# A two-layer decoder trunk on one core: two more expert tiles fetched ahead of a pass, and five gathered rows moved between passes

## The chip, the cores and the metric

The kernel runs on one core of one Trainium2 chip. Its time is the device time of one execution in microseconds (us); the median of three runs of the kernel before is 1489.36 us (1488.99 to 1492.16). Five engines work side by side, each through its own list of instructions in order: PE (matrix products), DVE (vector work), ACT (activations, copies, casts), POOL (here casts, and the issue of gathers) and SP (the issue of plain loads). All loads and gathers are carried by the core's 16 DMA engines.

## The reference

Two layers. Each has a mixer (layer 0: block-sparse attention and retention side by side; layer 1: a short gated convolution), and after it the expert retrieval "PEER", around which this change turns. The sequence has 256 tokens of 1024 numbers; u and v hold 16384 experts of 1024 numbers per layer.

```python
def peer(xn, w_q, sub_keys, u, v):
    ...
    q = (t @ w_q).reshape(n_tok, PEER_HEADS, 2, PEER_DKEY // 2)
    sc = jnp.einsum('thpd,hpnd->thpn', q, sub_keys).astype(jnp.float32)
    s1, i1 = lax.top_k(sc[:, :, 0], PEER_TOPK)
    s2, i2 = lax.top_k(sc[:, :, 1], PEER_TOPK)
    ...
    top_s, pos = lax.top_k(cand, PEER_TOPK)
    eidx = jnp.take_along_axis(cidx, pos, axis=-1)
    gate = jax.nn.softmax(top_s, axis=-1).astype(xn.dtype)
    ...
        hid = jax.nn.gelu(jnp.einsum('td,thkd->thk', tc, u[ec]), approximate=False)
        return jnp.einsum('thk,thkd->td', gc * hid, v[ec])

def reference(...):
    h = x
    for layer in range(DEPTH):
        xn = rmsnorm(h, norm_mix[layer])
        ...
        h = h + peer(rmsnorm(h, norm_ffn[layer]), peer_w_q[layer], peer_sub_keys[layer],
                     peer_u[layer], peer_v[layer])
    return rmsnorm(h, final_norm)
```

Each token has 8 heads with 16 experts each, 128 experts in all.

## The kernel before

**Two ways for two groups of tokens.** The first 96 tokens (`TG`) are served by gathering: for each of their 128 experts the row of u, and later the row of v, is fetched from memory by index. Since a gathered row-set spans 128 partitions and 96 of them are taken by a token each, the other 32 carry further experts of the same tokens, so that 96 row-sets (`STEPS`) of u and 96 of v are enough; the text calls a row-set of 128 x 1024 numbers a "row". The other 160 tokens (`TD`) are served densely: all 128 tiles of u (128 experts each) are multiplied with them, the result is passed through gelu, multiplied by a gate matrix G that is zero where an expert was not chosen, and multiplied with all 128 tiles of v. A row and a tile both have 512 KB.

**Stages of `peer`.** The queries (loop over `f`, 16 tiles of wq, L1260); the pass over u (loop over `i`, 128 tiles, L1388, products in `dense_u`); the pass over v (L1466). The top-16 selections go from the pump, a list of small DVE jobs that is drained a little after each query and each tile of u. When it is empty, the indices are transposed (`idx_tr`), and G is made in 40 groups of four tokens (`onehots`, `shared`, `g_mm`, `g_put`) between the products of u; from then on each tile's result is multiplied by the groups that are done (L1403), and `g_put` multiplies what had been computed before.

**Loads.** `Stream` loads the weights in the order of their use into eight buffers (`RAW`), each load as soon as the tile that had the buffer is used up; in the pass over v every second load is issued by ACT, all others by SP. `PRE` names 22 of the 128 tiles of u that do not go through the stream: the key is the tile's number, the value says which memory it is loaded into. 0 to 10 is the region of `HG` (the dense result, of which the rows of the first tiles are not written yet), 11 to 13 the three accumulators of the gather, 14 to 19 buffers that the queries leave (`uhi`, `ulo`, `one`, `xb`), and 20 and 21 that of the keys (`ko`). `fetch` issues such a load on SP: the 14 of `early` one after each query from the second on (L1277), the 8 of `early_u` one after each tile of u from the second on (L1392).

**The gather.** `Gather.issue` starts gathers on POOL (L975) as long as there is a free row buffer and the index is known: two buffers (`grow`) from the start, four more (`rows`) from `widen`, after the last query. The indices of the first third of the rows come from `places(0)`, those of the others from `places(1)`. `step` is called after each tile: it adds `ga.rate` to a credit, and for each whole credit consumes one row on DVE (L985: product with the token and sum, for u; L1002: multiply and add, for v) and issues the next gather. So the rate lays down in the program how many rows are consumed beside each tile:

```python
                ga.rate = (0.9 if 8 <= i < 46 else 0.6) if gst["g"] < 0 else (UPTO[l] - ga.c) / (NK - CALM - i) if i < NK - CALM else 0.6
                if i < NK - QUIET:
                    ga.step()
```

`gst["g"]` is below 0 until the transposition is done. `UPTO` is the number of rows (of 192 in a layer) that are to be consumed 11 tiles before the end of the pass over u; the others are spread over the pass over v. After each 32 rows of u their 32 columns of `hid` are passed through gelu on ACT (L991) and multiplied by their gates on DVE (L992), some rows later (`self.later`).

**The pass over v.** Of its 128 tiles 95 (`SPL`) are split in two parts, by a cast on ACT (L1378) and a subtraction on DVE (L1385), and multiplied with a split result (L1501, L1503); the other 33 are used whole (L1497).

The lists of the engines are fixed when the program is built; nothing is reordered on the chip, and an instruction that waits holds up what stands behind it on its engine.

Of the kernel before, what the change touches and what calls it, by code (L numbers as in the profile page):

```python
# [14 lines left out]
AF = mybir.ActivationFunctionType  # L15
OP = mybir.AluOpType
# [12 lines left out]
NK = 128  # L29
# [8 lines left out]
STEPS = TG  # L38
# [4 lines left out]
GT = 4  # L43
UNIT = 2.0 ** 15
SCR = 11 * D
UPTO = (112, 110)
SPL = [i for i in range(NK) if i % 2 or i % 4 == 0 and i > 0]
CODE = 64.0
WHOLE = 1.5 * 2.0 ** 23
PRE = {5 * k: k for k in range(11)} | {23: 20, 43: 21, 58: 14, 64: 15, 70: 11, 76: 16, 82: 18, 88: 12, 94: 17, 100: 13, 106: 19}  # L50
AHEAD = 3
QUIET = 4
CALM = 11
# [141 lines left out]
def trunk_kernel(ctx, tc, x, small, cst, mcst, ew_in, ew_out, ow_in, ow_out, wq, keys, pu, pv, pun, gains, out):  # L195
# [54 lines left out]
    def nm(s):  # L250
        uid[0] += 1
        return f"{s}{uid[0]}"
# [685 lines left out]
    class Gather:  # L938
# [9 lines left out]
        def __init__(self, pool):  # L948
            few = pool.tile([P, ROWS, D], F32, tag="grow", name=nm("grow"))
            self.rows = [few[:, i, :] for i in range(ROWS)]  # L950
            self.acc = [pool.tile([P, D], F32, tag=f"gacc{q}", name=nm("gacc")) for q in range(3)]
            self.hid = pool.tile([P, STEPS], F32, tag="ghid", name=nm("ghid"))
            self.known = 0
            self.rate = 0.0
            self.i = 0
            self.c = 0
            self.credit = 0.0
            self.later = {}
# [8 lines left out]

        def issue(self):

            while (self.i < self.TOTAL and (self.i < self.known or self.known == STEPS)  # L970
                   and self.i < self.c + len(self.rows)):
                s_ = self.i
                self.i += 1
                table = pun if s_ < STEPS else pv.rearrange("l i p d -> (l i p) d")
                gp.indirect_dma_start(self.row(s_), None, table,  # L975
                                      bass.IndirectOffsetOnAxis(IG[:, 0, s_ % STEPS:s_ % STEPS + 1].bitcast(U32), 0))

        def consume(self):
            s_ = self.c
            r = self.row(s_)  # L980
            j = s_ % STEPS
            q = j // SUB
            w = self.hid[:, j:j + 1]
            if s_ < STEPS:
                v.scalar_tensor_tensor(r, r, 1.0, XG[:, q % 2, :], op0=OP.mult, op1=OP.mult, accum_out=w)  # L985
                if s_ == SUB - 1:
                    gp.dma_start(XG[TG:, 0, :], XG[2 * SUB:TG, 0, :])
                if j % SUB == SUB - 1:
                    w = self.hid[:, q * SUB:(q + 1) * SUB]
                    g = IG[:, 1, q * SUB:(q + 1) * SUB]  # L990
                    self.later[s_ + 2] = lambda: act.activation(w, w, AF.Gelu)  # L991
                    self.later[s_ + 4] = lambda: v.tensor_tensor(w, w, g, OP.mult)  # L992
            elif j % SUB == 0:
                so_far = self.acc[q - 1] if q else h[:, 0, :]
                v.scalar_tensor_tensor(self.acc[q][:TG], r[:TG], w[:TG], so_far[:TG], op0=OP.mult, op1=OP.add)
                v.tensor_scalar(self.acc[q][TG:], r[TG:], w[TG:], None, op0=OP.mult)
                if q:
                    self.part(q - 1)
                if q == 2:
                    self.later[s_ + 8] = self.fold  # L1000
            else:
                v.scalar_tensor_tensor(self.acc[q], r, w, self.acc[q], op0=OP.mult, op1=OP.add)  # L1002
            self.later.pop(s_, lambda: None)()
            self.c += 1
# [17 lines left out]
    def peer(l, before, norm):  # L1022
        with tc.tile_pool(name=nm("hg"), bufs=1) as hp:
# [45 lines left out]
            def fetch(i):  # L1069

                k = PRE[i]
                if k < 11:
                    t = [flat[:, k * D:(k + 1) * D]]
                elif k < 14:
                    t = [ga.acc[k - 11]]
                elif 14 < k < 18:
                    t = [st.hi_pool.tile([P, D], F32R, tag="hi", name=nm("uhi")).bitcast(F32)]
                elif k > 19:  # L1080
                    if k == 20:
                        there["ko"] = new_ko().rearrange("p (a d) -> p a d", a=2)
                    t = [there["ko"][:, k - 20, :]]
                elif k == 18:
                    t = [Xb.rearrange("p k s -> p (k s)").bitcast(F32)]
                else:
                    n = 1 if k == 14 else 2
                    t = [st.lo_pool.tile([P, D], BF16, tag="lo", name=nm("ulo")).bitcast(F32) for _ in range(n)]
                    t += [one] * (2 - n)
                n = D // len(t)  # L1090
                for j, p in enumerate(t):
                    nc.sync.dma_start(p, pu[l, i][:, j * n:(j + 1) * n])
                there[i] = [p[:, c:c + P] for p in t for c in range(0, n, P)]

            there = {}
            early = [i for i in sorted(PRE) if PRE[i] < 14]
            early_u = [i for i in sorted(PRE) if PRE[i] >= 14]
            early_u = early_u[2:] + early_u[:2]
            pump = Pump()

# [154 lines left out]
            def chain(th, hf):  # L1255
                pump.add((1.0, stage2_build(th, hf)))
                pump.add(*[(2.2, stage2_top(th, a, a + 2)) for a in range(hf * HH, (hf + 1) * HH, 2)])
                pump.add(*extract(th, hf))

            for f in range(NPAIR):  # L1260
                if f == 0:
                    pair = u_pair(xv["x2"], Xb, before.tail)
                ps = pair[f] if f < 2 else u_tile(xv["x2"], Xb)
                act.copy(qT[f % 2], ps[:, :S])
                if f == 1:
                    rows = before.rows()
                if 1 < f < 6:
                    rows[f - 2]()
                if f:
                    scores(f - 1)  # L1270
                    pump.add((1.35, stage1(0, f - 1, f)))
                    if f <= HH * 2:
                        pump.add((1.35, stage1(1, f - 1, f)))
                    if f == HH * 2:
                        chain(0, 0)
                        pump.add((0.6, lambda: places(0)))
                    if early:  # L1277
                        fetch(early.pop(0))
                pump.run(3.2)
# [79 lines left out]
            def dense_u(i):  # L1359
                if i in PRE:  # L1360
                    w = there.pop(i)
                else:
                    t = st.next()
                    w = [t[:, k * P:(k + 1) * P] for k in range(ND)]
                ps = acc_tile(i % 4, nm("hid")) if i % 4 < 2 else hid_tile(nm("hid"))
                for k in range(ND):
                    pe.matmul(ps[:, :TD], w[k], XF[:, k, :], start=k == 0, stop=k == ND - 1)  # L1367
                    if k == ND // 2 - 1:
                        slot(i)
                return ps  # L1370
# [16 lines left out]
            first = st.nu + NK - len(PRE)  # L1387
            for i in range(NK):  # L1388
                ps = dense_u(i)
                if i == 0:  # L1390
                    after_first()
                elif early_u:  # L1392
                    fetch(early_u.pop(0))
                if i == NK - 1:
                    gst["rate"] = 1.0
                    while gst["g"] < NG:
                        slot(i)
                T = max(gst["g"], 0) * GT
                if T < TD:
                    act.activation(HG[:, i, T:], ps[:, T:TD], AF.Gelu)  # L1400
                if T > 0:
                    act.activation(ps[:, :T], ps[:, :T], AF.Gelu)
                    v.tensor_tensor(HG[:, i, :T], ps[:, :T], HG[:, i, :T], OP.mult)  # L1403
                slot(i + 1)
                if gst["g"] < 0:
                    if i == first_late - 2:
                        pump.flush()
                    if pump.q:
                        pump.run(1.4)
                    else:  # L1410
                        gst["g"] = 0
                        gst["rate"] = NG / (2.0 * (NK - 10 - i))
                        gst["credit"] = -0.6
                        xv["gate"] = new_ko(F16)
                        for g in range(3):
                            onehots(g)
                        todo += [0, 1]
                        shared()
                        shared()
                ga.rate = (0.9 if 8 <= i < 46 else 0.6) if gst["g"] < 0 else (UPTO[l] - ga.c) / (NK - CALM - i) if i < NK - CALM else 0.6  # L1420
                if i < NK - QUIET:
                    ga.step()
                elif i in (NK - QUIET, NK - QUIET + 2):
                    weight_parts(i - NK + QUIET + 1)
# [151 lines left out]
```

## Time and profile before

| | us |
|---|---|
| median of three runs | 1489.36 |
| the profiled execution, whole | 1490.58 |
| its span, first to last instruction | 1488.80 |
| around the span (difference) | 1.78 |
| layer 0: first query's products begin | 128.18 |
| layer 0: first tile of u begins | 182.53 |
| layer 0: first tile of v begins | 489.45 |
| layer 1: first tile of u begins | 907.24 |

| engine | busy, share of the span |
|---|---|
| PE (products) | 97% |
| PE (weight loads) | 90% |
| DVE | 84% |
| ACT | 51% |
| POOL | 50% |

Reading it: a stage's table gives, for a stretch of the span, each engine's busy time with its number of instructions, the clock that was granted to PE, the mean share in which the 16 DMA engines were busy (1.0 is full), and GB/s. In a list of waits, "A <- B: 10.9, 13, 1.5" says that A stood idle for B for 10.9 us in 13 waits, the longest 1.5. In a timeline a row has its start, its length, the engine and the line, what it writes and reads, how many instructions were merged, and in brackets the idle time before it and what ended it. In a table of groups stand busy time and mean ns of one, then the idle time before them. PE's busy time holds its pipelined products from begin to end, so a full PE is not PE at its peak. For products of u there are two instructions per 128 x 128 block, 16 per tile.

### The profile page before, as it was taken

What the parts mean: (1) busy time and instruction counts of PE and PEld (TensorE: products, weight loads), DVE (VectorE), ACT (ScalarE), POOL (GpSimd) and SP (SyncE); (2) the same over time, 40 slices, a digit from 0 to 9 for tenths busy, and PEclk for the clock granted to TensorE, in tenths of its full rate; (3) what the DMA queues carried; (4) which work ended last, traced back from release to release, by engine and by line L of the source; (5) the groups of instructions that cost most, each with busy time, mean ns of one, the idle gap of its engine ahead of it and who ended that gap; (6) DMA issues with size and microseconds to landing.
All of it is one profiled execution on the core that took longest, in us unless ns stands there. A gap on an engine that the chain in (4) does not pass through costs nothing.

```text
span 1488.8 us, 30108 instructions
## 1 busy us (share of the span) xinstructions
PE 1438.1 (97%) x11184; PEld 1334.8 (90%) x11184; DVE 1246.5 (84%) x2467; ACT 761.3 (51%) x1825; POOL 744.9 (50%) x513
## 2 busy tenths in 40 slices
PE   9999999999999999999989999999999999999997
PEld 5667999999999998889889799999999999988886
DVE  5637999879999788888876589996899978888888
ACT  6556511258875454445564463212888745454544
POOL 6754545546667243345335374453566643443532
PEclk9999999999999999999999999999999999999999
DMA  8545899999999999999966478999999999999995
GB/s 322 199 145 203 311 378 409 395 409 408 405 402 396 394 400 405 406 394 404 409 242 230 169 277 326 407 408 396 408 405 401 399 397 407 399 408 409 398 406 228
DMA packets 147618, 532.80 MB, mean 358 GB/s; under 512 B 16976, under 2 KB 17360, under 8 KB 147472
## 3 DMA queue, kind: packets, MB, share of 16 engines
q1 hardware_dynamic: 72288, 258.43, 44.9%
q0 software_dynamic: 56608, 204.81, 35.1%
q10 hardware_dynamic: 18576, 67.64, 11.5%
q8 instruction: 88, 1.44, 0.4%
q14 instruction: 58, 0.48, 0.1%
HBM read 528.40 MB, written 1.05 MB: 356 GB/s over the span
## 4 chain that ended last, share of the span: by engine, by line
PE 54%; issue 17%; POOL 11%; DMA 9%; DVE 7%; ACT 2%; POOLq 0%; DVEq 0%; ACTq 0%; SPq 0%
PE hid L1367 30%; POOL rows L975 7%; PE hid L261 5%; DMA raw<-pu 4%; DMA raw<-pv 3%; POOL grow L975 3%; PE hid L267 2%; PE G L1327 2%; DMA rows<-pv,ig 2%; PE ea L295 2%; PE vo L1501 2%; PE ea L294 2%; PE ea L293 2%; DVE gacc L1002 1%; PE vo L1497 1%
## 5 line engine op out<-in xcount | busy, mean ns | idle before, releaser
L1367 PE MATMUL hid<-xf,raw 128*128 128x160 f32 x3392 | 487.4, 301 | 7.3 <-DMA raw<-pu 4.6
L1367 PEld LDWEIGHTS hid<-xf,raw 128*128 128x128 f32 x3392 | 467.1, 191 | 10.5 <-issue 5.6
L1378 ACT CAST vhi<-raw 128x1024 fp32r<-128x1024 f32 x190 | 198.5, 1046 | 266.1 <-DMA raw<-pv 218.9
L975 POOL DMA_INDIRECT rows<-pv,ig x128 | 192.5, 1504 | 209.2 <-DVE gacc L1002 180.0
L1385 DVE TENSOR_TENSOR vlo<-raw,vhi 128x1024 bf16<-128x1024 f32 x190 | 231.9, 1223 | 77.4 <-ACT vhi L1378 69.1
L1501 PE MATMUL vo<-ko,vhi 128*128 128x320 f32 x1520 | 270.5, 320 | 24.5 <-DVE ko L1460 23.5
L1501 PEld LDWEIGHTS vo<-ko,vhi 128*128 128x128 f32 x1520 | 224.3, 188 | 33.8 <-DVE ko L1460 32.5
L975 POOL DMA_INDIRECT rows<-pun,ig x128 | 170.7, 1334 | 136.0 <-DVE rows L985 63.2
L151 POOL TENSOR_TENSOR lo<-raw,hi 128x1024 bf16<-128x1024 f32 x70 | 167.9, 2408 | 85.7 <-ACT hi L149 82.8
L985 DVE SCALAR_TENSOR_TENSOR rows<-rows,xg 128x1024 f32<-128x1024 f32 x128 | 155.5, 1220 | 22.5 <-DMA rows<-pun,ig 22.4
L1400 ACT ACTIVATE hg<-hid 128x160 f32<-128x160 f32 (+14 forms) x240 | 62.7, 265 | 199.1 <-PE hid L1367 199.0
L1002 DVE SCALAR_TENSOR_TENSOR gacc<-rows,ghid,gacc 128x1024 f32<-128x1024 f32 x124 | 158.8, 1281 | 4.7 <-DMA rows<-pv,ig 3.9
L975 POOL DMA_INDIRECT grow<-pv,ig x64 | 99.7, 1558 | 122.8 <-DVE gacc L1002 110.9
L1497 PE MATMUL vo<-hg,raw 128*128 128x160 f32 x1056 | 157.3, 302 | 1.0 <-DVE hg L1403 1.0
L1497 PEld LDWEIGHTS vo<-hg,raw 128*128 128x128 f32 x1056 | 145.5, 190 | 1.4 <-DVE hg L1403 1.4
L1503 PE MATMUL vo<-hb,vlo 128*128 128x160 bf16 x1520 | 138.1, 234 | 2.1 <-DVE vlo L1385 2.1
L1317 ACT ACTIVATE ko<-ko,idxT 128x128 f16<-128x128 f16 x320 | 101.8, 390 | 51.1 <-DVE ko L1303 50.9
L1503 PEld LDWEIGHTS <-vlo 128*128 128x128 bf16 x1520 | 100.5, 98 | 22.1 <-DVE vlo L1385 3.1
L975 POOL DMA_INDIRECT grow<-pun,ig x64 | 81.3, 1270 | 77.6 <-DVE grow L985 43.3
L149 ACT CAST hi<-raw 128x1024 fp32r<-128x1024 f32 x100 | 102.8, 1046 | 30.0 <-PE hid L261 18.5
L261 PE MATMUL hid<-x,hi 128*128 128x256 f32 x800 | 107.4, 287 | 0.2 <-DVE cg L912 0.2
L1320 ACT ACTIVATE ko<-ko,idxT 128x128 f16<-128x128 f16 x320 | 101.1, 388 | 0.0
(251 smaller groups left out, 2097.2 us busy)
## 6 DMA issues: line engine op xcount, KB each, us to landing
raw<-pu SPq DMA_DIRECT2D x212, 512.0 KB, 7.9
raw<-pv SPq DMA_DIRECT2D x128, 512.0 KB, 8.9
raw<-pv ACTq DMA_DIRECT2D x128, 512.0 KB, 8.0
raw<-wq SPq DMA_DIRECT2D x32, 512.0 KB, 3.9
raw<-ew_in SPq DMA_DIRECT2D x28, 512.0 KB, 4.5
raw<-ow_in SPq DMA_DIRECT2D x24, 512.0 KB, 5.3
hg<-pu SPq DMA_DIRECT2D x22, 512.0 KB, 5.1
raw<-ew_out SPq DMA_DIRECT2D x8, 512.0 KB, 3.1
```

The source lines that it names most:

```text
L149: self.nc.scalar.copy(hi, t)
L151: eng.tensor_tensor(lo, t, hi.bitcast(F32), OP.subtract)
L261: pe.matmul(ps[:, :S], hi[:, k * P:(k + 1) * P], A2[:, k, s_, :], start=k == 0 and s_ == 0, stop=False)
L975: gp.indirect_dma_start(self.row(s_), None, table, bass.IndirectOffsetOnAxis(IG[:, 0, s_ % STEPS:s_ % STEPS + 1].bitcast(U32), 0))
L985: v.scalar_tensor_tensor(r, r, 1.0, XG[:, q % 2, :], op0=OP.mult, op1=OP.mult, accum_out=w)
L1002: v.scalar_tensor_tensor(self.acc[q], r, w, self.acc[q], op0=OP.mult, op1=OP.add)
L1367: pe.matmul(ps[:, :TD], w[k], XF[:, k, :], start=k == 0, stop=k == ND - 1)
L1378: act.copy(whi[j], raw)
L1385: v.tensor_tensor(wlo[j], raw, whi[j].bitcast(F32), OP.subtract)
L1497: pe.matmul(vo[b][:, :TD], w[:, b * P:(b + 1) * P], HG[:, i, :], stop=False, **m)
L1501: pe.matmul(vo[b][:, :2 * TD], hi[:, b * P:(b + 1) * P], hs, stop=i == NK - 1, **m)
L1503: pe.matmul(vo[b][:, :TD], lo[:, b * P:(b + 1) * P], hb, stop=i == NK - 1, **m)
```

## The change

Five edits, alike in both layers.

1. `PRE` gets two more tiles: tile 1 and tile 2 of u, with the values 22 and 23, are loaded into the first two row buffers of the gather (`ga.rows[0]` and `[1]`, which are `grow`). They leave the stream, and belong to `early`, which now has 16 loads; three of these (tiles 0, 1, 2) are asked for ahead of the first query, the other 13 one after each query from the second on.
2. `Gather.held`: no gather is issued until tile 2 of u is done, since the first two row buffers hold tiles 1 and 2 until then.
3. The loads of `early_u` are all issued after the first tile of u, not one after each tile.
4. `UPTO` is 117 and 115 in place of 112 and 110, and the rate in the stretch of tiles 8 to 45 is 0.93 in place of 0.9.
5. Gelu and gate product of a third of the rows stand 12 and 16 rows after its last row, not 2 and 4.

```diff
@@ -43,11 +43,11 @@
 GT = 4
 UNIT = 2.0 ** 15
 SCR = 11 * D
-UPTO = (112, 110)
+UPTO = (117, 115)
 SPL = [i for i in range(NK) if i % 2 or i % 4 == 0 and i > 0]
 CODE = 64.0
 WHOLE = 1.5 * 2.0 ** 23
-PRE = {5 * k: k for k in range(11)} | {23: 20, 43: 21, 58: 14, 64: 15, 70: 11, 76: 16, 82: 18, 88: 12, 94: 17, 100: 13, 106: 19}
+PRE = {5 * k: k for k in range(11)} | {1: 22, 2: 23, 23: 20, 43: 21, 58: 14, 64: 15, 70: 11, 76: 16, 82: 18, 88: 12, 94: 17, 100: 13, 106: 19}
 AHEAD = 3
 QUIET = 4
 CALM = 11
@@ -951,6 +951,7 @@
             self.acc = [pool.tile([P, D], F32, tag=f"gacc{q}", name=nm("gacc")) for q in range(3)]
             self.hid = pool.tile([P, STEPS], F32, tag="ghid", name=nm("ghid"))
             self.known = 0
+            self.held = True
             self.rate = 0.0
             self.i = 0
             self.c = 0
@@ -967,7 +968,7 @@
 
         def issue(self):
 
-            while (self.i < self.TOTAL and (self.i < self.known or self.known == STEPS)
+            while (not self.held and self.i < self.TOTAL and (self.i < self.known or self.known == STEPS)
                    and self.i < self.c + len(self.rows)):
                 s_ = self.i
                 self.i += 1
@@ -988,8 +989,8 @@
                 if j % SUB == SUB - 1:
                     w = self.hid[:, q * SUB:(q + 1) * SUB]
                     g = IG[:, 1, q * SUB:(q + 1) * SUB]
-                    self.later[s_ + 2] = lambda: act.activation(w, w, AF.Gelu)
-                    self.later[s_ + 4] = lambda: v.tensor_tensor(w, w, g, OP.mult)
+                    self.later[s_ + 12] = lambda: act.activation(w, w, AF.Gelu)
+                    self.later[s_ + 16] = lambda: v.tensor_tensor(w, w, g, OP.mult)
             elif j % SUB == 0:
                 so_far = self.acc[q - 1] if q else h[:, 0, :]
                 v.scalar_tensor_tensor(self.acc[q][:TG], r[:TG], w[:TG], so_far[:TG], op0=OP.mult, op1=OP.add)
@@ -1077,6 +1078,8 @@
                     t = [ga.acc[k - 11]]
                 elif 14 < k < 18:
                     t = [st.hi_pool.tile([P, D], F32R, tag="hi", name=nm("uhi")).bitcast(F32)]
+                elif k > 21:
+                    t = [ga.rows[k - 22]]
                 elif k > 19:
                     if k == 20:
                         there["ko"] = new_ko().rearrange("p (a d) -> p a d", a=2)
@@ -1093,8 +1096,8 @@
                 there[i] = [p[:, c:c + P] for p in t for c in range(0, n, P)]
 
             there = {}
-            early = [i for i in sorted(PRE) if PRE[i] < 14]
-            early_u = [i for i in sorted(PRE) if PRE[i] >= 14]
+            early = [i for i in sorted(PRE) if not 14 <= PRE[i] < 22]
+            early_u = [i for i in sorted(PRE) if 14 <= PRE[i] < 22]
             early_u = early_u[2:] + early_u[:2]
             pump = Pump()
 
@@ -1257,6 +1260,8 @@
                 pump.add(*[(2.2, stage2_top(th, a, a + 2)) for a in range(hf * HH, (hf + 1) * HH, 2)])
                 pump.add(*extract(th, hf))
 
+            for _ in range(3):
+                fetch(early.pop(0))
             for f in range(NPAIR):
                 if f == 0:
                     pair = u_pair(xv["x2"], Xb, before.tail)
@@ -1387,10 +1392,13 @@
             first = st.nu + NK - len(PRE)
             for i in range(NK):
                 ps = dense_u(i)
+                if i == 2:
+                    ga.held = False
+                    ga.issue()
                 if i == 0:
                     after_first()
-                elif early_u:
-                    fetch(early_u.pop(0))
+                    for j in early_u:
+                        fetch(j)
                 if i == NK - 1:
                     gst["rate"] = 1.0
                     while gst["g"] < NG:
@@ -1417,7 +1425,7 @@
                         todo += [0, 1]
                         shared()
                         shared()
-                ga.rate = (0.9 if 8 <= i < 46 else 0.6) if gst["g"] < 0 else (UPTO[l] - ga.c) / (NK - CALM - i) if i < NK - CALM else 0.6
+                ga.rate = (0.93 if 8 <= i < 46 else 0.6) if gst["g"] < 0 else (UPTO[l] - ga.c) / (NK - CALM - i) if i < NK - CALM else 0.6
                 if i < NK - QUIET:
                     ga.step()
                 elif i in (NK - QUIET, NK - QUIET + 2):
```

## The prediction

> **What bounds the kernel now.** I read the stages first (busy time by stretch), then who waits for whom inside them, then the order of events at the one place where the stretches show a hole. "Layer 0" and "layer 1" are the two channel mixers; each has queries (16 tiles of wq), a pass over u (128 tiles, `i` at L1388) and a pass over v (128 tiles, L1466). The stretches are, in layer 0: the end of the mixer and the first queries, the end of the queries, u before the gate matrix G, u with G in two parts, v. Three of layer 1 follow.
>
> ```profile
> core 0: us, PE busy (x) PEld busy (x) DVE busy (x) ACT busy (x) POOL busy (x), PEclk, DMA share, GB/s
> 130.00:140.00 10.00, 9.77 (x84) 9.15 (x83) 7.53 (x29) 7.67 (x18) 6.24 (x5) 1.00 0.28 106
> 140.00:178.00 38.00, 37.38 (x323) 35.75 (x323) 35.97 (x162) 22.04 (x45) 27.21 (x14) 1.00 0.90 322
> 178.00:190.00 12.00, 12.00 (x98) 11.79 (x97) 11.35 (x30) 4.74 (x12) 2.52 (x4) 1.00 0.62 232
> 190.00:310.00 120.00, 117.85 (x855) 117.43 (x854) 108.67 (x380) 22.37 (x64) 58.02 (x53) 0.99 1.03 404
> 310.00:410.00 100.00, 100.00 (x842) 99.08 (x840) 90.81 (x169) 79.32 (x299) 60.18 (x43) 1.00 1.03 407
> 410.00:480.00 70.00, 68.13 (x563) 66.32 (x562) 68.54 (x105) 48.87 (x193) 49.90 (x31) 1.00 1.02 399
> 560.00:740.00 180.00, 169.50 (x1404) 158.27 (x1403) 154.85 (x142) 87.88 (x110) 79.07 (x53) 1.00 1.02 404
> ...
> 853.00:860.00 7.00, 6.76 (x53) 5.84 (x52) 5.96 (x15) 5.87 (x14) 2.68 (x5) 1.00 0.02 5
> 903.00:915.00 12.00, 12.00 (x97) 11.82 (x95) 11.31 (x32) 4.75 (x12) 2.53 (x5) 1.00 0.61 225
> 915.00:1034.00 119.00, 116.58 (x856) 115.94 (x855) 108.22 (x377) 22.52 (x64) 56.17 (x51) 1.00 1.03 403
> ```
>
> From 190 to 740 us the DMA engines have no gap: share 1.02 to 1.03, about 404 GB/s. The holes lie ahead of it: 106 GB/s at 130 (5 at 853 in layer 1), and 232 and 225 GB/s in the 12 us in which the queries end and u begins. A tile of u or v and a gathered row-set are both 512 KB, so each costs 524,288 B / 404 GB/s = **1.30 us** of the engines. PE is full in u as well: it works 217.85 of the 220 us from 190 to 410, its one gap among them; in v (560 to 740) it lacks 10.5 us of 180. Who is waited for, in u from 200 and in v of layer 0 (us in total, times, longest), then in layer 1's u before G and its v:
>
> ```profile
> PE hid L1367 <- DMA raw<-pu: 2.1, 2, 1.9
> PE hid L1367 <- DVE hg L1403: 1.8, 4, 0.8
> PE vo L1501 <- DVE ko L1460: 10.9, 13, 1.5
> PE vo L1503 <- DVE vlo L1385: 1.8, 1, 1.8
> DVE vlo L1385 <- ACT vhi L1378: 31.9, 34, 2.3
> ...
> PE hid L1367 <- DMA raw<-pu: 2.4, 3, 2.1
> PE vo L1501 <- DVE ko L1460: 11.6, 14, 1.4
> ...
> L1378 ACT CAST vhi<-raw 128x1024 fp32r<-128x1024 f32 x190 | 198.5, 1046 | 266.1 <-DMA raw<-pv 218.9
> ```
>
> In v PE waits for DVE, DVE for ACT's cast, and that cast for the transfer of v: 218.9 of its 266.1 idle us. So **v is bound by DMA**, u by PE with DMA just keeping up, and PE loses 2.1 and 2.4 us once per layer at a late tile of u.
>
> **The change part by part.** *Three loads ahead of the queries* (tiles 0, 1, 2; two of them new in the first row buffers). Their target is free when the mixer's last product is done, about 128.2 us; SP has nothing else to issue there:
>
> ```profile
> 128.18 1.50 PE L278 MATMUL hid<-x,hi 128*128 128x256 f32 x8
> 135.33 2.58 SPq L134 DMA_DIRECT2D raw<-wq  x2
> 138.01 0.38 SPq L1092 DMA_DIRECT2D hg<-pu  x1
> ...
> 178.43 0.38 SPq L1092 DMA_DIRECT2D ulo<-pu  x1
> 187.53 0.33 SPq L134 DMA_DIRECT2D raw<-pu  x1
> 187.90 0.43 SPq L1092 DMA_DIRECT2D uhi<-pu  x1
> 202.28 0.33 SPq L1092 DMA_DIRECT2D ko<-pu  x1
> ```
>
> Behind these three issues (about 0.4 us each) in SP's queue stand the two loads of wq of 135.33, which wait for other things until then; 3 x 1.30 = 3.9 us of transfer fits into 128 to 135. Cost 0; if that cover went, a query would wait up to 3.9 us. Thirteen more loads then go between the queries instead of thirteen after the first, at the same pace. So by 178 two tiles more have arrived: **2.6 us of DMA moved out of the full stretch**, per layer.
>
> *Late-free buffers at once.* Before, the second of these loads comes at 187.90 and the last at 202.28, each behind a load of raw that waits for PE. After, all are issued behind one another as their buffers come free: hi and lo with the last queries (by 182), ko when the last scores are done (185). The raw loads behind them lose nothing: the first now belongs to tile 3, whose end is at 182.53 + 0.45 + 4 x 2.17 = 191.7 us (first rows of the next view: a tile each (193.85 - 185.16) / 4 = 2.17, and the scores between the first two). The hole can take (404 - 232) x 12 us = 2.06 MB, 3.9 tiles (layer 1: 178 x 12 = 4.1). Bounds: 0 (they come no earlier) and 3.9; I take **3**, since ko is free only at 185 and seven tiles, 9.1 us, are ready to fill 179 to 190.
>
> ```profile
> 182.53 2.34 PE L1367 MATMUL hid<-xf,hg 128*128 128x160 f32 x16
> 185.16 8.86 PE L1367 MATMUL hid<-xf,raw 128*128 128x160 f32 x64
> 193.85 2.34 PE L1367 MATMUL hid<-xf,hg 128*128 128x160 f32 x16
> 224.65 6.26 PE L1367 MATMUL hid<-xf,raw 128*128 128x160 f32 x32 [1.90 <-DMA raw<-pu]
> ...
> 189.00 1.02 POOL L975 DMA_INDIRECT grow<-pun,ig  x1 [0.91 <-DVE hg L1106]
> ```
>
> *Gathers held until i = 2.* Tile 2 ends at 182.53 + 0.45 + 3 x 2.17 = 189.5; the first gather went at 189.00, because its places were not known earlier. Held back 0.5 us on POOL, and nothing but gathers is queued there: 0. With eight tiles of backlog gone or early at 190, the wait at 222.7 (tiles loaded late behind six gathers and eight loads) should go: **-2.1 and -2.4 us**. Bounds 0 and those; I take all.
>
> *Five rows from v to u.* In v, 5 x 1.30 = **-6.5 us** per layer while PE keeps 10.9 + 1.8 us of waits there to give back (11.6 in layer 1). In u, one of the five is consumed before the index transposition (in the order of the programs 45 rows stand before it, formerly 44; 0.93 for 0.9), four after it. What they meet there, all on DVE, 310 to 490 us:
>
> ```profile
> L1303 DVE TENSOR_TENSOR ko<-cst,idxT 128x1024 f16<-128x1024 f32 x40 | 48.7, 1222 | 0.0
> L985 DVE SCALAR_TENSOR_TENSOR rows<-rows,xg 128x1024 f32<-128x1024 f32 x36 | 43.8, 1224 | 7.0 <-DMA rows<-pun,ig 6.9
> L985 DVE SCALAR_TENSOR_TENSOR grow<-grow,xg 128x1024 f32<-128x1024 f32 x17 | 20.8, 1222 | 3.0 <-DMA grow<-pun,ig 3.0
> L1002 DVE SCALAR_TENSOR_TENSOR gacc<-rows,ghid,gacc 128x1024 f32<-128x1024 f32 x12 | 15.4, 1283 | 0.1
> ```
>
> Four rows are 4 x 1.25 = 5.0 us of DVE. In 310 to 410 DVE idles 9.2 of 100 us, in 410 to 480 only 1.5 of 70, and there PE already waits 1.8 us for L1403. By share of time 2.1 us of the 5.0 fall into the full part and pass to PE; the other 2.9 us pass only if the waits for rows (6.9 + 3.0) stay. Bounds 1 and 5 us; I take **+3.1**, the middle.
>
> *Gelu and gate product 10 and 12 rows later.* The weights are first read by row 96, while the first third is now ready at row 47: 0. Cover gone: one wait of DVE on L992, whose own time is 0.2 us.
>
> **Sum.** Layer 0: -2.1 - 6.5 + 3.1 = -5.5; layer 1: -2.4 - 6.5 + 3.1 = -5.8; together **-11.3 us**. The check by bytes: where DMA never rests the end moves by what arrives before 190: 2 + 3 tiles, -6.5 us per layer, -13.0, less what DMA idles anew because PE or DVE holds it; -15.3 with the whole hole filled. The two agree within 2 us. The profiled execution took 1490.58 us (span 1488.80 and 1.78 around it), which gives 1479.3; the median of the runs, 1489.36, is 1.22 below it: 1478.1, said as **1478.5**.
>
> The Trainium skill, "HBM Reference", Specifications (TRN2) and Access, gives a core about 358 GB/s as its share and about 425 alone. By the share a tile would be 1.46 us and five rows 7.3, by the other 1.23 and 6.2 (an estimate from that page), so the sum would be -13.0 or -10.6; the 404 GB/s of the rows above decide, and lie between.
>
> **The rivals.** *Only the new tiles count.* The hole at 178 stays (SP waits for lanes or PE), and five rows in u are paid in u: -2.6 per layer, 1484. For it: SP issues in order and ko hangs on PE. Against: seven tiles are free by 182 to 185.
>
> *The rows' price in u is v's gain.* If all 5.0 us of DVE and 1.30 of DMA per row pass to PE, and the early wait stays since PE's loads still queue behind six gathers: -6.5 + 6.5 = 0; 1489. Against: the 2.1 us wait comes of a backlog that is started 10 us earlier.
>
> *The round trip of a row becomes the bound; slower.* Six buffers; a row goes round in emission on POOL, landing, consumption:
>
> ```profile
> 377.91 1.68 POOL L975 DMA_INDIRECT rows<-pun,ig  x1 [1.00 <-DVE rows L985]
> 381.84 0.94 POOL L975 DMA_INDIRECT grow<-pun,ig  x1 [0.30 <-issue]
> DMA to landing us min/median/max: 6.3/11.5/16.2
> ...
> DVE rows L985 <- DMA rows<-pun,ig: 9.5, 11, 1.3
> DVE grow L985 <- DMA grow<-pun,ig: 6.0, 5, 2.1
> ```
>
> Median 11.5 + 1.3 = 12.8 us, over six 2.13 us per row. From the transposition on u takes 117 - 45 = 72 rows, some 70 of them from 310 to 480, in 170 us: 2.4 us each, so it holds as long as the trip is under 14.6 us. Past that every row is late: at 15.5 (landing 14.2) u grows by 70 x 15.5 / 6 - 170 = 11 us, against a gain of 8.6: **1494**. For it: layer 1 already waits 15.5 us for rows with G. Against: the backlog that makes landing long starts smaller at 190. The Trainium skill, "SBUF — State Buffer", SBUF: two separate sides, says that GpSimd cannot write descriptors while DVE holds the shared port. By that rule the emission would lengthen with a fuller DVE; the trace shows 1.68 us beside 0.94, and which DVE operation makes it, no row shows.
>
> **How the numbers follow.** Forecast (-7 to -15 us) 0.55; only the tiles (-3 to -7) 0.2; no change 0.1; slower 0.15. What a measurement here can tell from no change is about 0.2%, 3 us: faster 0.75, same 0.10, slower 0.15. The low end is -15.3 us, 1474; the high end, 1488, reaches nearly to the no-change case and leaves out the slower one. The forecast's own range is 1474 to 1482.
>
> **What would show it.** Right: over 350 GB/s at 178 to 190 and traffic at 128 to 135; no wait of L1367 for raw<-pu near 222; u's end earlier or later by no more than 2 us against its beginning; v shorter by 5 to 7 us; the wait for L1403 at 3 to 6 us. Wrong: a DVE that waits more than 10 us for rows beside G, a query that waits for wq, or a v whose PE waits stay at 12 us.

## The result, and the profile after

| | before | after |
|---|---|---|
| median of the runs, us | 1489.32 (6 runs, 1488.97 to 1492.16) | 1480.15 (6 runs, 1476.77 to 1481.2) |
| ratio, 95% interval | | 0.9935 [0.9925, 0.9945] |
| the profiled execution, whole | 1490.58 | 1481.2 |
| its span | 1488.80 | 1479.4 |

The changed kernel is faster by 0.65%, 9.2 us; 1478.5 was forecast. Two later series gave 0.9948 [0.9935, 0.9960] and 0.9924 [0.9911, 0.9938] for the same kernel. These two lie 0.24%, 3.6 us, apart, so a difference of that size between kernels of different series is not to be read from these runs.

Where the 9.4 us of the two spans went is read from the timeline: the first product of u, the first of v, and the last of v. First the kernel before (layer 0's first two starts, 182.53 and 489.45, and layer 1's u, 907.24, stand in the table above), then after, PE rows alone:

```profile
755.84 0.73 PE L1503 MATMUL vo<-hb,vlo 128*128 128x160 bf16 x8
...
1211.81 2.06 PE L1497 MATMUL vo<-hg,raw 128*128 128x160 f32 x14
...
1475.31 0.73 PE L1503 MATMUL vo<-hb,vlo 128*128 128x160 bf16 x8
```

```profile
182.86 2.34 PE L1372 MATMUL hid<-xf,hg 128*128 128x160 f32 x16
...
491.61 2.06 PE L1505 MATMUL vo<-hg,raw 128*128 128x160 f32 x14
...
751.10 0.73 PE L1511 MATMUL vo<-hb,vlo 128*128 128x160 bf16 x8
...
902.74 2.34 PE L1372 MATMUL hid<-xf,hg 128*128 128x160 f32 x16
...
1209.09 2.06 PE L1505 MATMUL vo<-hg,raw 128*128 128x160 f32 x14
...
1465.92 0.73 PE L1511 MATMUL vo<-hb,vlo 128*128 128x160 bf16 x8
```

| us | before | after | difference | forecast |
|---|---|---|---|---|
| start to u, layer 0 | 182.53 | 182.86 | +0.33 | 0 |
| u, layer 0 | 306.92 | 308.75 | +1.83 | -2.1 + 3.1 |
| v, layer 0 | 267.12 | 260.22 | -6.90 | -6.5 |
| v's end to u, layer 1 | 150.67 | 150.91 | +0.24 | 0 |
| u, layer 1 | 304.57 | 306.35 | +1.78 | -2.4 + 3.1 |
| v, layer 1 | 264.23 | 257.56 | -6.67 | -6.5 |
| after v | 12.76 | 12.75 | 0 | 0 |

The whole gain stands in v, and u is longer: by this table the five rows came cheap. The experiments show that it gives the gain to the wrong edit.

The stages of after (busy time by stretch; columns as before; the two of layer 1 lie 4.5 and 5 us earlier than those of before, since its u begins 4.5 us earlier):

```profile
130.00:140.00 10.00, 9.75 (x82) 9.13 (x82) 7.52 (x27) 7.34 (x17) 6.25 (x5) 1.00 0.67 237
...
178.00:190.00 12.00, 12.00 (x98) 11.76 (x98) 11.35 (x29) 4.45 (x11) 1.52 (x3) 1.00 0.95 347
190.00:202.00 12.00, 12.00 (x90) 12.00 (x90) 11.14 (x60) 1.22 (x4) 5.76 (x6) 1.00 0.88 313
190.00:310.00 120.00, 117.38 (x852) 117.14 (x852) 111.36 (x384) 21.77 (x61) 65.68 (x55) 0.99 1.01 396
...
848.50:855.50 7.00, 6.77 (x53) 5.84 (x52) 5.95 (x15) 5.87 (x14) 2.69 (x5) 1.00 0.64 229
898.00:910.00 12.00, 12.00 (x98) 11.76 (x97) 11.35 (x29) 4.54 (x12) 1.52 (x3) 1.00 0.99 371
```

The first hole is used (237 GB/s, before 106; layer 1 229, before 5), and the second is nearly full (347, before 232; layer 1 371, before 225). But right behind it is a hole that was not there: 313 GB/s from 190 to 202, where before had 403 (this row of before is taken from the same view):

```profile
190.00:202.00 12.00, 12.00 (x90) 12.00 (x89) 11.17 (x58) 1.53 (x6) 5.20 (x7) 1.00 1.02 403
```

Who is waited for in after, in u of layer 0 up to 490 us, in v of layer 0 (560 to 740) and of layer 1 (1300 to 1460), and then, in a fence of its own, the group of the cast in v over the whole span:

```profile
DVE rows L986 <- DMA rows<-pun,ig: 3.3, 6, 0.7
...
PE hid L1372 <- ACT hg L1408: 2.6, 1, 2.6
...
PE hid L1372 <- DVE hg L1411: 2.5, 4, 0.8
...
PE vo L1509 <- DVE ko L1468: 6.4, 8, 1.4
...
PE vo L1509 <- DVE ko L1468: 6.2, 7, 2.1
```

```profile
L1383 ACT CAST vhi<-raw 128x1024 fp32r<-128x1024 f32 x190 | 198.7, 1046 | 253.3 <-DMA raw<-pv 184.0 <-DVE gacc L1003 23.7 <-PE vo L1509 22.5
```

The wait for raw<-pu is gone from u. PE's wait for DVE in layer 0's v (490 to 756 us) fell from 10.9 to 6.4 us, and the cast's wait for transfers of v from 218.9 to 184.0. A single wait of 2.6 us for ACT is new. Three rows of the timeline show it, ACT first, then PE:

```profile
292.79 0.31 ACT L1212 ACTIVATE hg<-hg 128x128 f32<-128x128 f32 x1 [7.70 <-DVE hg L1201]
293.11 1.28 ACT L1408 ACT_TABLE_LOAD   x1
294.41 0.89 ACT L1408 ACTIVATE hg<-hid 128x160 f32<-128x160 f32 x4
```

```profile
294.76 4.11 PE L1372 MATMUL hid<-xf,hg 128*128 128x160 f32 x16 [2.62 <-ACT hg L1408]
...
1014.56 4.12 PE L1372 MATMUL hid<-xf,hg 128*128 128x160 f32 x16 [2.55 <-ACT hg L1408]
```

L1212 is the exponential of the second gates (`gates_exp(1)`), placed in ACT's list by the pump. It stands 7.70 us for DVE, four results of u queue behind it for gelu, and PE runs out of places for its next product. In before the same instruction waited 2.69 us, and PE did not feel it.

### The profile page after: what moved, and what is told of

The parts are those of the page before. It is cut to its first block, busy times and chain, and to the rows that moved or that the text cites. A ratio compares the mean times of both kernels' runs of the same rounds, so it can differ in the third digit from the quotient of the medians.

```text
span 1479.4 us, 30103 instructions
## 1 busy us (share of the span) xinstructions
PE 1436.0 (97%) x11184; PEld 1337.0 (90%) x11184; DVE 1244.3 (84%) x2467; ACT 762.8 (52%) x1825; POOL 745.8 (50%) x513
## 4 chain that ended last, share of the span: by engine, by line
PE 38%; DVE 25%; issue 19%; POOL 11%; DMA 4%; ACT 2%; POOLq 0%; SPq 0%; DVEq 0%; ACTq 0%
PE hid L1372 19%; POOL rows L976 8%; POOL grow L976 4%; DVE rows L986 4%; PE hid L261 3%; DMA rows<-pv,ig 2%; PE G L1332 2%; DVE grow L986 2%; DVE hg L1109 2%; DVE hg L1115 2%; DVE hg L1111 2%; DMA raw<-pv 2%; PE ea L295 2%; PE ea L294 2%; PE ea L293 2%
## 5 line engine op out<-in xcount | busy, mean ns | idle before, releaser
L1372 PE MATMUL hid<-xf,raw 128*128 128x160 f32 x3328 | 476.6, 300 | 4.3 <-DVE hg L1411 3.7
L1372 PEld LDWEIGHTS hid<-xf,raw 128*128 128x128 f32 x3328 | 456.8, 190 | 7.0 <-DVE hg L1411 5.5
L1383 ACT CAST vhi<-raw 128x1024 fp32r<-128x1024 f32 x190 | 198.7, 1046 | 253.3 <-DMA raw<-pv 184.0
L976 POOL DMA_INDIRECT rows<-pv,ig x128 | 187.5, 1464 | 226.6 <-DVE gacc L1003 188.9
L976 POOL DMA_INDIRECT rows<-pun,ig x128 | 177.1, 1383 | 121.6 <-DVE rows L986 70.4
```

Source lines behind the costliest of these rows:

```text
L976: gp.indirect_dma_start(self.row(s_), None, table, bass.IndirectOffsetOnAxis(IG[:, 0, s_ % STEPS:s_ % STEPS + 1].bitcast(U32), 0))
L1383: act.copy(whi[j], raw)
```

## The experiments

Each ratio is to the kernel before in runs of the same chip. Unless said otherwise an edit is made to the changed kernel.

### The rows alone, and all but the rows

To before: `UPTO = (117, 115)` and 0.93, nothing else.

> The kernel before with edit 4 alone (117 and 115 rows by the end of u, rate 0.93), no load moved. Theory (the gain comes of the bytes that are moved into the hole before 190 us, and the rows only let v use it): DMA is already full in u, so u grows by about what v loses, 6.5 us per layer: 1487 to 1492 us. Rival (u had room for five more rows, and v shortens by itself): 2 x (-6.5 + 1 to 3) us, 1479 to 1483 us, all of the change's gain.

1491.11 us, ratio 1.0015 [1.0004, 1.0025]. The rows alone bring no gain, rather a loss of 0.15%. Layer 0's v was 8.4 us shorter (258.73), its u 8.5 longer (315.42). The waits from 190 to 490 us in this kernel:

```profile
DVE rows L985 <- DMA rows<-pun,ig: 9.7, 9, 1.4
...
PE hid L1367 <- DVE hg L1403: 7.0, 8, 1.7
...
DVE grow L985 <- DMA grow<-pun,ig: 5.3, 7, 1.3
...
PE hid L1367 <- DMA raw<-pu: 1.9, 1, 1.9
```

DVE waits 15.0 us for rows here (18.4 in before), and PE waits 7.0 us for DVE at L1403 instead of 1.8.

```diff
-UPTO = (117, 115)
+UPTO = (112, 110)
-                ga.rate = (0.93 if 8 <= i < 46 else 0.6) ...
+                ga.rate = (0.9 if 8 <= i < 46 else 0.6) ...
```

> The changed kernel with edit 4 undone (112 and 110 rows, rate 0.9): tiles, hold, loads at once stay. Theory: the wait for raw<-pu at 222 us goes (2.1 and 2.4 us), the wait of PE at 292 us for ACT stays or shrinks, DMA gets slack in u which v cannot use in full: 1482 to 1487 us. Rival (loads add nothing): 1488 to 1490 us.

1481.09 us, ratio 0.9949 [0.9935, 0.9962]; its interval overlaps those of the whole change. Better than expected: the edits that are left, those of the loads above all, carry nearly all. Its waits, in u up to 490 us and in v (560 to 740):

```profile
PE hid L1372 <- ACT hg L1408: 1.4, 1, 1.4
...
PE vo L1509 <- DVE ko L1468: 11.5, 12, 1.7
```

u takes 301.03 us in both layers, without a wait for DVE, and v keeps its old 266.01 and 263.71. So the loads' gain falls to u where the five rows stay in v, and moving the rows passes it on to v: against this kernel the changed one has +7.7 and +5.3 us in u, -5.8 and -6.2 in v.

### The wait for ACT

One idle entry of the pump's list is moved ahead of the second exponential, so that it is issued later.

```diff
-                pump.add((0.3, lambda: gates(1)), (3.0, None), (0.0, lambda: gates_exp(1)), (3.0, None),
-                         (0.6, lambda: gates_norm(1)), (3.0, None), (3.0, None), (0.5, idx_tr), (3.0, None))
+                pump.add((0.3, lambda: gates(1)), (3.0, None), (3.0, None), (0.0, lambda: gates_exp(1)), (3.0, None),
+                         (0.6, lambda: gates_norm(1)), (3.0, None), (0.5, idx_tr), (3.0, None))
```

> The changed kernel with the second exponential of the gates on ACT two or three tiles later (one empty step of the pump moved from behind it to before it), the transposition where it was. In the changed kernel ACT waits 7.7 us for DVE there and PE 2.6 us per layer behind ACT. Theory A (u is bound by PE, v's length by its own transfers): both waits of 2.6 us go and the end with them, 1474.5 to 1476.5 us. Theory B (from 190 to 740 us the bytes alone set the end): the 2.6 us come back as later waits in u or v, 1479 to 1481 us.

1479.46 us, ratio 0.9938 [0.9924, 0.9951]: no difference from the changed kernel. The wait itself went, and came back as one for DVE (waits of 190 to 490 us; after had 2.5 here):

```profile
PE hid L1372 <- DVE hg L1411: 5.0, 6, 1.7
```

u took 308.23 us instead of 308.75. Taking away the visible wait is worth nothing here: the next one takes its place.

More than the wait went with it. Behind PE's longest wait of u the clock granted to it (the column ahead of the DMA share) was lower for a few microseconds: the wait for raw<-pu at 222 in before, the wait for ACT at 292 in after, and the same stretch in this kernel without that wait:

```profile
222.00:230.00 8.00, 6.10 (x33) 5.88 (x32) 7.93 (x31) 0.61 (x2) 3.67 (x5) 0.79 1.03 411
```

```profile
294.00:302.00 8.00, 7.24 (x41) 7.24 (x42) 6.58 (x14) 1.90 (x7) 5.55 (x5) 0.79 1.03 410
```

```profile
294.00:302.00 8.00, 8.00 (x61) 8.00 (x60) 6.11 (x13) 1.64 (x7) 7.08 (x4) 1.00 1.03 410
```

A clock of 0.79 over 8 us is 1.7 us of PE's full speed (an estimate from these rows). With the wait of 2.6 us, PE got back some 4.3 us here, and u became only 0.5 us shorter (308.23, against 308.75, 310.73 and 308.64 in the three profiles of after): the end of u does not follow PE's time alone.

### The burst

```diff
-                    for j in early_u:
-                        fetch(j)
+                elif early_u:
+                    fetch(early_u.pop(0))
```

> The changed kernel with edit 3 undone: the eight loads into late-free buffers one after each tile of u again. Theory: the hole of 178 to 190 us stays (about 230 GB/s), three to four tiles per layer are back in the full stretch, and the wait for raw<-pu near 222 us is back: 4 to 5 us per layer lost by bytes, 2 to 2.5 by that wait: 1484 to 1489 us. Rival (the two tiles ahead of the queries carry it): within 1 us of 1480.

1486.78 us, ratio 0.9984 [0.9973, 0.9996]: without the burst most of the gain is lost; 0.16% is left of the changed kernel's 0.52 to 0.76%. The hole at 178 is back in the stages, and the one from 190 to 202 stays, though the first gather goes at 189.33 here:

```profile
178.00:190.00 12.00, 12.00 (x98) 11.80 (x98) 11.35 (x30) 4.75 (x12) 2.19 (x4) 1.00 0.60 222
190.00:202.00 12.00, 12.00 (x91) 12.00 (x90) 11.14 (x59) 1.50 (x5) 5.08 (x6) 1.00 0.88 316
```

The wait for raw<-pu near 222 did not come back, against the expectation; PE lost 4.9 us in the wait for ACT instead.

The reverse, before with this edit alone:

> The kernel before with edit 3 alone: the loads of early_u all issued after the first tile of u. Theory (bytes left at 190 us set the end): the hole at 178 to 190 goes from 232 to about 345 GB/s, worth (345 - 232) x 12 us = 1.36 MB or 2.6 tiles, 3.4 us per layer; the index copies land some 5 us after their issue behind the burst, the first gather moves from 189.0 to about 193, and part of it is given back at 192 to 200: 1482 to 1486. Rival (the burst pays only with the tiles fetched ahead of the queries, since without them the first loads of raw queue behind it and PE waits): 1488 to 1492, with a wait of L1367 for raw<-pu above 2 us in the first 40 us of u.

1485.10 us, ratio 0.9969 [0.9959, 0.9979]: the burst pays by itself, without tiles ahead of the queries. Layer 0's two stretches show no second hole:

```profile
178.00:190.00 12.00, 12.00 (x98) 11.82 (x96) 11.31 (x32) 4.75 (x12) 1.52 (x3) 1.00 1.00 384
190.00:202.00 12.00, 12.00 (x91) 12.00 (x90) 10.79 (x54) 1.52 (x5) 5.91 (x7) 1.00 1.03 409
```

In its profiled execution all of the gain lies in layer 0 (5.4 us from the first product of u to the last of v); layer 1 took 569.07 us there, 568.80 before, though its hole was filled too. There u became 2.4 us shorter and v 2.6 us longer. Why layer 1 gained nothing is open; with the tiles ahead of the queries, in the three profiles of after, it gained 4.9, 2.9 and 3.5.

### The two tiles and the hold

Tiles 1 and 2 stay in the stream, and nothing is held (`held = False` from the start); the three loads ahead, the burst and the rows stay.

> The changed kernel without its two new tiles and without the hold (three loads still ahead of the queries, loads at once, 117 and 115 rows). Bytes theory: 2.6 us per layer are lost with the tiles, and 2.7 us won with gathers that start at 189 us again: 1479 to 1482 us, so the tiles pay for little more than their own hold. Rival (as forecast: the hold costs nothing): 1484.5 to 1486.5 us.

1482.66 us, ratio 0.9945 [0.9929, 0.9961], beside the changed kernel's 1482.76 in the same series: the two tiles and their hold make no difference that these runs show. That is near the first theory's time, but not for its reason. The first gather goes at 193.09 us without any hold, where after had 193.79. POOL's rows of the timeline, of after and of this kernel, and the copies of the indices that the gather needs (DMA issues of 180 to 200 us, median time to landing last), of before and of this kernel:

```profile
186.91 1.52 POOL L1226 DMA_DIRECT2D ig<-hg  x3 [9.56 <-DVE ig L1227]
193.79 1.02 POOL L976 DMA_INDIRECT grow<-pun,ig  x1 [5.36 <-DVE hg L1115]
```

```profile
193.09 1.02 POOL L976 DMA_INDIRECT grow<-pun,ig  x1 [4.90 <-DVE hg L1113]
```

```profile
ig<-hg POOLq DMA_DIRECT2D x3, 4.0 KB, 1.6
```

```profile
ig<-hg POOLq DMA_DIRECT2D x3, 4.0 KB, 5.5
```

Three copies of 4 KB took 1.6 us to land where the engines had a hole and 5.5 behind the burst. That this delays the gathers is read from the order in six kernels: the first gather goes at 189.00 where the copies took 1.6 us, at 192.22 where they took 4.6, at 192.33 with 5.1, and from 192.75 to 193.12 with 5.5 and 5.6. Without the burst, with the hold, it went at 189.33. So the hold costs nothing, as forecast, but the burst delays the gathers by some 4 us.

The late gathers alone do not open the hole from 190 to 202: the burst alone has its first gather at 192.75 and 409 GB/s there, and the kernel without the burst has 316 with its first gather at 189.33. What differs is SP's next load of the stream. It goes into a buffer of `RAW`, and so waits for PE to be done with a tile of the stream (without the burst it stood 11.9 us for PE, up to 191.82 us). In before it was asked for at 187.53 us; SP's first loads of raw after 178 us in after, without the two tiles, and with the burst alone:

```profile
192.20 19.89 SPq L134 DMA_DIRECT2D raw<-pu  x8
```

```profile
187.62 24.23 SPq L134 DMA_DIRECT2D raw<-pu  x10
```

```profile
187.32 24.23 SPq L134 DMA_DIRECT2D raw<-pu  x10
```

Tiles 1 and 2 leave the stream, so its first buffer comes free two tiles later, after tile 3, and until then nothing new is asked for. What the two tiles bring early is for the most part missing there: without them the stretch from 190 to 202 has 345 GB/s, with them 313 (309 and 326 in the other two profiles of after). A part of the hole is there without them too, and what makes that part is open. By 202 us the engines had moved 24.15, 24.40 and 24.54 MB since 120 us in the three profiles of after, 24.13 MB without the two tiles, and 22.15 MB in before.

Another kernel let the gathers begin in the four wide buffers and dropped the hold after the last query:

> The changed kernel with the gathers beginning in the four wide row buffers, so that the hold is not needed: they are issued right after the last query, and only the fifth and sixth meet tiles 1 and 2. In the changed kernel the first gather goes at 193.8 us, not at 189.5 as forecast, and DMA is at 313 GB/s from 190 to 202 us (403 before). Bytes theory: that second hole is 91 GB/s x 12 us, 2.1 tiles, 2.7 us per layer, and comes off the end: 1473.5 to 1476.5 us. Rival (u is held by DVE and PE, earlier rows only wait longer in their buffers): 1479 to 1481 us.

1513.83 us, ratio 1.0164 [1.0151, 1.0177]. Here the gathers stand in the program ahead of the products of tiles 1 and 2, so that these products read gathered rows in place of the two tiles of u, and waited for them:

```profile
204.25 6.56 PE L1373 MATMUL hid<-xf,grow 128*128 128x160 f32 x32 [18.92 <-DMA grow<-pun,ig]
```

It doesn't answer its question. Its first gather, at 192.33 us, agrees with the reading above.

The last try was to shorten the burst ahead of the copies:

```diff
-                    for j in early_u:
+                    for j in early_u[:-2]:
                         fetch(j)
+                elif i in (4, 5):
+                    fetch(early_u[i - 6])
```

> The changed kernel with the last two of the late-free loads, those into ko, issued after tiles 4 and 5 of u instead of after tile 0. Theory (the first gathers wait for the copies of the indices, and these queue behind the burst): the copies land 2 to 3 us after issue instead of 5.5, the first gather goes at 190 to 191.5 instead of 193.8, the hole at 192 to 196 is filled: 1 to 2 us less per layer, ratio to before 0.991 to 0.993. Rival (two tiles of transfer are only moved from one hole to the other, or the gathers wait for something else): first gather at 193 or later, ratio 0.9935 to 0.995.

1483.21 us, ratio 0.9948 [0.9933, 0.9962], beside the changed kernel's 1479.30 in the same series. The theory missed: the copies landed after 4.6 us, the first gather went at 192.22, and the engines had run dry by then. By stretches of 2 us:

```profile
186.00:188.00 2.00, 2.00 (x17) 2.00 (x16) 1.84 (x10) 1.52 (x3) 1.52 (x3) 1.00 1.02 415
188.00:190.00 2.00, 2.00 (x17) 2.00 (x16) 1.83 (x11) 0.30 (x1) 0.00 (x0) 1.00 0.66 238
190.00:192.00 2.00, 2.00 (x17) 2.00 (x16) 1.83 (x10) 0.30 (x1) 0.00 (x0) 1.00 0.02 4
192.00:194.00 2.00, 2.00 (x17) 2.00 (x16) 1.86 (x10) 0.25 (x1) 1.48 (x2) 1.00 0.75 205
```

SP's next load is one of raw at 191.57, when PE is done with tile 3, and the two loads of ko stood behind it. So the two tiles served better as cover for the copies' landing; that this is the whole of the 3.9 us between the two medians is not shown, as the intervals overlap.

### Gelu and gate product, and the same kernel again

Edit 5 undone (2 and 4 rows in place of 12 and 16):

> The changed kernel with edit 5 undone (gelu 2 and gate product 4 rows after each third). Forecast and bytes theory: no more than 1 us from the changed kernel, 1479 to 1481.5 us. Rival (ACT is held at the gelu until the row of DVE comes, with the activations of u behind it, as it is at the exponential): 2 to 3 us per layer more, 1484 to 1486 us.

1479.86 us, ratio 0.9933 [0.9920, 0.9946]: the edit brings and costs nothing. The changed kernel twice more:

> The changed kernel once more, on the chip and beside the runs of these experiments: 1479 to 1481 us by every theory.

1482.76 us, ratio 0.9948 [0.9935, 0.9960], first gather at 193.12 us.

> The changed kernel once more, as the measure for the two others of this call. Both theories: ratio to before 0.993 to 0.995, first gather at 193.8 us.

1479.30 us, ratio 0.9924 [0.9911, 0.9938], first gather at 192.87. No version that was tried is faster than the changed kernel by more than these series differ among themselves.

## Why the prediction was right, step by step

**What bounds the kernel: right for v and for the bytes, not for u.** The prediction had u bound by PE, with DMA just keeping up, and took its sum from that. But DMA is full from the first gathers to the end of v (share 1.02, 401 to 404 GB/s from 202 to 750 in all versions of the table), so the end moves in the main by the bytes that arrive before. The mean rate over both holes and what lies between them, before and then after:

```profile
120.00:202.00 82.00, 80.84 (x637) 74.89 (x637) 73.30 (x290) 40.88 (x91) 44.52 (x30) 1.00 0.73 270
```

```profile
120.00:202.00 82.00, 80.83 (x636) 74.61 (x636) 72.92 (x291) 40.63 (x90) 44.14 (x29) 1.00 0.83 295
```

The table sets this rate beside layer 0's length from the first product of u to the last of v in one profiled execution, each against before, and beside the ratio of all runs, which holds both layers. "By bytes" is (rate - 270) x 82 us / 404, an estimate.

| version | GB/s, 120 to 202 | by bytes, layer 0, us | measured, layer 0, us | ratio of all runs |
|---|---|---|---|---|
| before | 270 | 0 | 0 (574.04) | 1 |
| rows alone | 271 | -0.2 | +0.1 | 1.0015 |
| no burst | 275 | -1.0 | -3.2 | 0.9984 |
| last two loads late | 291 | -4.3 | -1.0 | 0.9948 |
| burst alone | 294 | -4.9 | -5.4 | 0.9969 |
| no tiles 1 and 2 | 294 | -4.9 | -1.9 | 0.9945 |
| after, three profiles | 295, 298, 299 | -5.1, -5.7, -5.9 | -5.1, -4.0, -4.4 | 0.9935, 0.9948, 0.9924 |
| no rows | 298 | -5.7 | -7.0 | 0.9949 |
| exponential later | 299 | -5.9 | -6.2 | 0.9938 |
| gelu early | 300 | -6.1 | -4.7 | 0.9933 |

By the ratios, the account parts the two versions that bring few bytes from the others, and it comes within some 3 us of one profiled execution; the order among the others it does not give. Part of its misses is the one execution that was profiled: those of the late loads and of the kernel without the tiles were the slowest of their series (1485.51 and 1485.48 us), that of no burst the fastest of its eleven (1484.39). The full stretch is also not at quite one rate: 401 and 402 GB/s from 202 to 750 in the first two, 404 in no burst, 403 in before, and 1 GB/s over 548 us is 1.4 us (an estimate). PE's clock is a further candidate: from 294 to 302 it was 0.57 in the late loads and 0.79 without the tiles, against 1.00 in no rows and exponential later. No run separates these. The burst alone stays the exception: in layer 0 it gains what its bytes say, in layer 1 nothing, though the rate was 292 GB/s there (839.3 to 921.3 us; 267 in before at the same distance from u), and by the ratio it gains 0.31%, not 0.52 to 0.76%.

**Three loads ahead of the queries: right that they cost nothing, wrong in what the two new tiles are worth.** There are 237 GB/s at 130, and u's start is later by 0.33 and 0.24 us at most. From 120 to 178 us 16.24 MB came, 14.52 in before: 3.3 tiles more, where two were named. But the prediction said of the stream's loads that they lose nothing, the next one being due when tile 3 ends, at 191.7 us. It came at 192.20, against 187.53 in before, and in that time the lead was lost: without the two tiles nearly as much had come by 202, and the runs took the same time. The 2.6 us per layer that the byte check books for them are not shown.

**Late-free buffers at once: 3 tiles taken, 2.6 came** ((347 - 232) GB/s x 12 us = 1.38 MB; 347 is just under the 350 that the prediction named as a sign, and layer 1 had 371). This is the edit that pays, alone (0.9969) and by its absence (0.9984). What the prediction missed is the next stretch: (403 - 313) x 12 = 1.08 MB, 2.1 tiles, is given back from 190 to 202. The byte check of -13.0 us becomes about -11 by the rows of after: -5.1 in layer 0, and -6.3 in layer 1, where the rate was 267 GB/s in before (844.7 to 926.7 us) and 298 in after (840.2 to 922.2). Measured were -9.4.

**Gathers held until i = 2: right in its price of the hold, wrong in its time.** 189.5 was forecast and 193.79, 193.12 and 192.87 came in the three profiles; the copies of the indices, which the step did not look at, land behind the burst.

**The wait for raw<-pu: right that it goes, wrong that its 2.1 and 2.4 us are won in u.** The wait for ACT took 2.62 and 2.55 us in its place, and where that was removed a wait for DVE did. From 410 to 480 DVE works 68.74 of 70 us in after and DMA has no gap, and one wait fewer only lets the next one show.

**Five rows from v to u: right in size, wrong in meaning.** v gave 6.90 and 6.67 us (6.5 forecast). In u the wait for L1403, now L1411, rose by 0.7 us in layer 0, not to the 3 to 6 us that were named; still u grew by 1.8 us, against +1.0 and +0.7 from the prediction's two terms. (The +3.1 is called the middle of 1 and 5; that is 3.0.) Against the kernel without the rows, u grew by 7.7 and 5.3 us, near the rival "the rows' price in u is v's gain", which the rows alone confirm (+8.5 and -8.4). What carries the -9.2 us are the loads, nearest to the byte account that stood beside the sum as a check. The loads shorten u by 5.9 and 3.5 us (the kernel without the rows against before), and the rows lengthen it again by a little more and shorten v. So the sum by stages, with -6.5 for the rows as its largest term, came out by luck: the time that the rows move is nearly equal to what the loads had won.

**Gelu and gate product later: right**, 0. **The round trip of a row** did not become the bound: DVE's waits for rows in layer 0's u fell from 18.4 to 3.8 us; with the rows alone they were 15.0, so it is the loads' edits that go with the fall. Why is not shown.

## What to carry to other kernels

Where DMA is full to the end, count the bytes that arrive before the full stretch begins as a first estimate (here good to some 3 us in layer 0; for the burst alone it fails in layer 1), and give no credit for moving a transfer from one full stage to another: the move shows up as a gain in one stage and a loss in the next. Where loads are moved ahead, ask when the next one can be asked for, since a buffer that is free later opens the next hole. Where a hole is filled with a burst, look at what small transfer is issued behind it and who waits for that; and where a wait is removed in a stage in which several engines are near full, expect the next one in its place.

## What the runs showed of the hardware

Copies of 4 KB, issued by POOL, landed 1.6 us after their issue into idle DMA engines and 5.5 us after it into full ones. With two tiles less ahead of them they still took 4.6 us. Of the 96 packets of under 512 bytes that their queue moved then, 90 went from 188.5 to 190 us, as the loads ahead of them ran out (share of the engines 0.91, 0.32 and 0.11 in three half microseconds), and the last six up to 191. With the burst alone 94 of the 96 moved from 190 to 192, beside loads that held the engines full (412 GB/s); the two loads into ko, asked for at 185.14 us, ahead of them, took 8.5 us to land. The Trainium skill, "DMA: Bandwidth & Descriptors", Queues, rings and completion order, says that an engine takes turns between the queues it has work for, packet by packet. By that rule a short transfer on POOL's queue would not wait for the whole backlog of SP's, and with the burst alone it did not; still it landed 3.9 us later than into idle engines. Whether by the arbitration or by the time that each small packet takes when the engines are full, no row here tells.

ACT's change from exponential to gelu took 1.28 us (293.11 to 294.39), and the first gelu began 0.02 us later.

Behind single waits of PE of 1.9 to 4.4 us in u the granted clock was lower for up to 8 us: 0.79 from 222 to 230 in before, behind 1.9 us; 0.79 from 294 to 302 in after, behind 2.6; 0.57 there with the last two loads late, behind 4.4. With the burst alone a wait of 2.1 us stood at the same place and the clock stayed at 1.00, so the length of the wait alone does not settle it.
